# Backward of log-softmax: thirty-two groups in straight code, against two groups and a loop of fifteen rounds

## The chip, the cores and the metric

The kernel runs on one core of a Trainium2 chip. The metric is the device time of one execution in microseconds, median of several. All runs told here were at a granted clock of 1.0; executions of one kernel mostly lie within 0.1% of one another. SyncE issues all transfers, ACT (ScalarE) and DVE (VectorE) compute.

## The reference, cut to what matters

```python
y, dy: float32 [8, 1024, 8192]
softmax_x = np.exp(y)
sum_dy = np.sum(dy, axis=-1, keepdims=True)
return (dy - softmax_x * sum_dy).astype(np.float32)
```

## The kernel before

8192 rows are taken in 32 groups of 128 partitions x 2 rows, so a group is 128 x 16384 floats, 8.39 MB, and a partition's part of it is one run of 64 KiB. Two dy buffers (x0, x1) and one y buffer that two groups share with an offset hold two groups at a time; groups therefore go in pairs A, B. The Python loop unrolls to straight code. The part that matters:

```python
    def sums(j):                       # -sum(dy) of both rows: one on DVE, one on ACT
        ...
    def compute(j, at, pieces, in_psum):
        for b, e in pieces:
            ...                        # ACT: exp of a piece of y, in place or into PSUM
            ...                        # DVE: x = exp * (-sum) + x, in place

    for g in range(0, G, 2):
        load_dy(g, 0)                  # dy A -> x0
        load_y(g, SHIFT)               # y A
        sums(0)
        compute(0, SHIFT, EXP_A, (IN_PSUM, IN_PSUM + Q))
        load_dy(g + 1, 1)              # dy B -> x1
        sums(1)
        load_y(g + 1, 0)               # y B, over most of y A
        store(g, 0, 0, W)              # store A
        for r in range(R):
            compute(1, 0, EXP_B[3 * r : 3 * r + 3], ())
            store(g + 1, 1, r * D, (r + 1) * D)   # store B, in two halves
```

## Time and profile before

| | before |
|---|---|
| time, median | 1867.8 us |
| span in the profile | 1865.8 us |
| bytes moved / mean rate | 805.31 MB / 432 GB/s |
| transfers' share of 16 DMA engines | 99.8% |
| DVE / ACT busy | 46% / 37% |
| dy load, issue to landing (median) | 47.9 us |

The lines for these stand in the prediction. A transfer of 8.39 MB needs 19.4 us at this rate, yet takes 47.9 us from issue to landing: the difference is time in the queue. One further pair of lines is needed below, from the timeline of the kernel before at its very start (start us, duration us): the only moment at which a load meets an empty queue.

```profile
0.73 0.38 SPq L61 DMA_DIRECT2D x<-in_dy_dram  x1
...
22.50 8.69 DVE L72 TENSOR_REDUCE stats<-x 128x1 f32<-128x8192 f32 x1 [22.50 <-DMA x<-in_dy_dram]
```

It was issued at 0.73 and had landed at 22.50: 21.8 us, 2.4 us more than its bytes need.

### The profile page before, as it was taken

The numbers are of one execution on the slowest core, as the hardware profiler recorded it, in microseconds if no ns is written. First come the engines' busy times: TensorE is split into PE (matmuls) and PEld (weight loads), VectorE is DVE, ScalarE is ACT, GpSimd is POOL, SyncE is SP. The second block draws the span as 40 slices with busy tenths as digits, with TensorE's granted clock in tenths as the row PEclk, the third lists the DMA queues.
The fourth block names the chain that finished last, engine by engine and source line by source line (L and its number), as shares of the span: only waits on it lengthen the run. The fifth ranks groups of instructions, "written<-read, shape, count | busy, mean of one in ns | idle before, by whom it ended". The sixth has DMA issues, their size and how long they took to land.

```text
span 1865.8 us, 920 instructions
## 1 busy us (share of the span) xinstructions
DVE 860.6 (46%) x288; ACT 689.0 (37%) x273; POOL 0.2 (0%) x4
## 2 busy tenths in 40 slices
DVE  2717427173271732717327173271733716337163
ACT  2606326053260532605326053260533605335053
POOL 0000000000000000000000000000000000000000
DMA  9999999999999999999999999999999999999998
GB/s 427 427 427 427 433 444 427 431 444 421 435 441 434 429 430 441 430 430 441 430 431 440 431 432 434 436 430 431 441 430 430 436 436 431 433 440 426 433 437 377
DMA packets 16135, 805.37 MB, mean 432 GB/s; under 512 B 1792, under 2 KB 1792, under 8 KB 1792
## 3 DMA queue, kind: packets, MB, share of 16 engines
q1 hardware_dynamic: 16128, 805.31, 99.8%
q14 instruction: 7, 0.06, 0.0%
HBM read 536.87 MB, written 268.44 MB: 432 GB/s over the span
## 4 chain that ended last, share of the span: by engine, by line
DMA 56%; DVE 18%; ACT 12%; another core or an unknown queue 10%; issue 2%; SPq 0%; ACTq 0%; DVEq 0%
DMA x<-in_dy_dram 30%; DMA y_t<-in_y_dram 26%; DVE x L96 18%; ACT y_t L92 6%; ACT x L75 6%; SPq L67 0%; ACTq L142 0%; DVEq L142 0%; SPq L61 0%; SPq L64 0%; ACTq L92 0%; ACTq L75 0%
## 5 line engine op out<-in xcount | busy, mean ns | idle before, releaser
L96 DVE SCALAR_TENSOR_TENSOR x<-y_t,stats,x 128x1024 f32<-128x1024 f32 (+2 forms) x192 | 511.1, 2704 | 396.1 <-ACT y_t L92 394.7
L72 DVE TENSOR_REDUCE stats<-x 128x1 f32<-128x8192 f32 x32 | 277.9, 8683 | 589.9 <-DMA x<-in_dy_dram 589.9
L92 ACT ACTIVATE y_t<-y_t 128x3072 f32<-128x3072 f32 (+6 forms) x176 | 403.7, 2362 | 393.6 <-DMA y_t<-in_y_dram 393.6
L75 ACT ACTIVATE x<-x 128x8192 f32<-128x8192 f32 x32 | 225.0, 7030 | 757.4 <-DMA x<-in_dy_dram 732.8
L96 DVE SCALAR_TENSOR_TENSOR x<-e_t,stats,x 128x2048 f32<-128x2048 f32 x32 | 73.7, 2345 | 0.0
L92 ACT ACTIVATE e_t<-y_t 128x2048 f32<-128x2048 f32 x32 | 58.5, 1858 | 0.0
L75 ACT ACTIVATION_READ_ACCUMULATOR x<-x 128x1 f32 x32 | 6.0, 187 | 0.0
L76 DVE TENSOR_SCALAR stats<-stats 128x1 f32<-128x1 f32 x32 | 4.6, 145 | 0.0
L75 ACT ACT_TABLE_LOAD x1 | 1.3, 1283 | 0.7 <-PEq L131 0.7
L131 POOL MEMSET const-bfloat16-1.0<- 128x1 bf16 x1 | 0.1, 102 | 0.0
L131 POOL MEMSET const-uint8-127<- 128x1 uint8 x1 | 0.1, 101 | 0.0
L131 POOL MEMSET const-float32-0.0<- 128x1 f32 x1 | 0.1, 99 | 0.2 <-issue 0.2
L131 POOL MEMSET const-float32-1.0<- 128x1 f32 x1 | 0.1, 98 | 0.0
## 6 DMA issues: line engine op xcount, KB each, us to landing
out_dram<-x SPq DMA_DIRECT2D x32, 4096.0 KB, 18.3
x<-in_dy_dram SPq DMA_DIRECT2D x32, 47.9
y_t<-in_y_dram SPq DMA_DIRECT2D x32, 34.6
out_dram<-x SPq DMA_DIRECT2D x16, 38.2
```

Source lines behind the costliest of these rows:

```text
L72: nc.vector.tensor_reduce(out=stats[:, c : c + 1], in_=x[:, :D], axis=mybir.AxisListType.X, op=ALU.add, negate=True)
L75: nc.scalar.activation(x[:, D:], x[:, D:], COPY, accum_out=stats[:, c + 2 : c + 3])
L76: nc.vector.tensor_scalar(out=stats[:, c + 1 : c + 2], in0=stats[:, c + 2 : c + 3], scalar1=-1.0, scalar2=None, op0=ALU.mult,)
L92: nc.scalar.activation(e_ap, y_t[:, at + b : at + e], EXP)
L96: nc.vector.scalar_tensor_tensor(out=x[:, lo:hi], in0=e_ap[:, lo - b : hi - b], scalar=stats[:, 4 * j + r : 4 * j + r + 1], in1=x[:, lo:hi ...
L131: nc = _bacc.Bacc("TRN2", target_bir_lowering=False, num_devices=1)
```

## The change

The intent is a short program at the same speed: the first pair stays straight code, the other fifteen are rounds of one loop. The loop resets its semaphores stage by stage, so that engines need not all meet at the branch (a barrier there instead made it 1935.2 us and not 1867.6, as run barrier shows below). The author cut the loop body into four stages, lets ACT and DVE report a stage finished at the start of the next one (`done_early`), and declares the three stores independent, since with a register in the address the compiler can't see it.

```diff
-    for g in range(0, G, 2):
-        load_dy(g, 0)
-        load_y(g, SHIFT)
+    def done_early():
+        for engine in (mybir.EngineType.Activation, mybir.EngineType.DVE):
+            tc.previous_stage_wait(engine)
+
+    def two_groups(h, boundary, early):
+        load_dy(h, 0)
+        load_y(h, 0, SHIFT)
+        boundary()
+        early()
         sums(0)
         compute(0, SHIFT, EXP_A, (IN_PSUM, IN_PSUM + Q))
-        load_dy(g + 1, 1)
+        load_dy(h, 1)
+        boundary()
+        early()
         sums(1)
-        load_y(g + 1, 0)
-        store(g, 0, 0, W)
-        for r in range(R):
-            compute(1, 0, EXP_B[3 * r : 3 * r + 3], ())
-            store(g + 1, 1, r * D, (r + 1) * D)
+        load_y(h, 1, 0)
+        compute(1, 0, EXP_B, ())
+        boundary()
+        stores = [store(h, 0, 0, W), store(h, 1, 0, D), store(h, 1, D, W)]
+        for k, later in enumerate(stores):
+            for earlier in stores[:k]:
+                tc.declare_no_dep(later.ins, earlier.ins, reason="different parts of out")
+
+    two_groups(0, lambda: None, lambda: None)
+    with tc.For_i(1, G // 2, 1, iteration_sync="staggered") as h:
+        two_groups(h, tc.stage_boundary, done_early)
```

(The cut parts give the views of y, dy and out a second index for A and B.)

More of the change, by code (lines that the diff above doesn't have):

```diff
@@ L47 @@
     assert D <= IN_PSUM
-    y_v = y.flatten_outer_dims().rearrange("(g p r) d -> g p (r d)", p=P, r=R)
-    dy_v = dy.flatten_outer_dims().rearrange("(g p r) d -> g p (r d)", p=P, r=R)
-    out_v = out.flatten_outer_dims().rearrange("(g p r) d -> g p (r d)", p=P, r=R)
+    y_v = y.flatten_outer_dims().rearrange("(h j p r) d -> h j p (r d)", j=2, p=P, r=R)
+    dy_v = dy.flatten_outer_dims().rearrange("(h j p r) d -> h j p (r d)", j=2, p=P, r=R)
+    out_v = out.flatten_outer_dims().rearrange("(h j p r) d -> h j p (r d)", j=2, p=P, r=R)
     pool = ctx.enter_context(tc.tile_pool(name="pool", bufs=1))
@@ L58, with load_dy, load_y, store @@
     stats = pool.tile([P, 8], fp32, name="stats")
-    def load_dy(g, j):
-        nc.sync.dma_start(out=x_ts[j][:], in_=dy_v[g])
-    def load_y(g, at):
-        nc.sync.dma_start(out=y_t[:, at : at + W], in_=y_v[g])
-    def store(g, j, lo, hi):
-        nc.sync.dma_start(out=out_v[g][:, lo:hi], in_=x_ts[j][:, lo:hi])
+    def load_dy(h, j):
+        nc.sync.dma_start(out=x_ts[j][:], in_=dy_v[h, j])
+    def load_y(h, j, at):
+        nc.sync.dma_start(out=y_t[:, at : at + W], in_=y_v[h, j])
+    def store(h, j, lo, hi):
+        return nc.sync.dma_start(out=out_v[h, j][:, lo:hi], in_=x_ts[j][:, lo:hi])
     def sums(j):
```

## The prediction

> **What bounds the kernel now.** I read four views in this order: the busy rows of the page, the list of transfers, what the transfer-issuing queue waited for, and one pair of groups on the timeline.
>
> The busy rows and the slices come first (engine, busy us, share, instructions; then the mean busy share and rate of the 16 DMA engines in 40 slices).
>
> ```profile
> span 1865.8 us, 920 instructions
> DVE 860.6 (46%) x288; ACT 689.0 (37%) x273; POOL 0.2 (0%) x4
> ...
> DMA  9999999999999999999999999999999999999998
> DMA packets 16135, 805.37 MB, mean 432 GB/s; under 512 B 1792, under 2 KB 1792, under 8 KB 1792
> q1 hardware_dynamic: 16128, 805.31, 99.8%
> ```
>
> The reader is to see that neither compute engine passes half the span while the DMA engines are busy 99.8% of it. 805.31 MB is the least that can move: three tensors of 8 x 1024 x 8192 x 4 = 268.4 MB, two read and one written. At 432 GB/s that is 1864 us of the 1866. So nothing can be gained except by a higher rate, and a loss needs one thing only: a moment when the transfer queue is empty.
>
> The question is therefore how much transfer work is still queued whenever SyncE issues the next transfer. One group of 128 x 16384 floats is 8.39 MB, 19.4 us at 432 GB/s; half a group is 9.7 us. Here is SyncE's issuing over one steady pair (start us, duration us, line, operation; L61 loads dy, L64 loads y, L67 stores):
>
> ```profile
> 916.06 0.33 SPq L67 DMA_DIRECT2D out_dram<-x  x1
> 916.44 0.77 SPq L61 DMA_DIRECT2D x<-in_dy_dram  x1
> 917.30 0.73 SPq L64 DMA_DIRECT2D y_t<-in_y_dram  x1
> 934.45 0.33 SPq L61 DMA_DIRECT2D x<-in_dy_dram  x1
> 984.32 0.33 SPq L64 DMA_DIRECT2D y_t<-in_y_dram  x1
> ```
>
> and from the same stretch of the compute engines' timeline, when data landed (the end of the idle time in brackets is the landing):
>
> ```profile
> 953.80 7.03 ACT L75 ACTIVATE x<-x 128x8192 f32<-128x8192 f32 x1 [43.71 <-DMA x<-in_dy_dram]
> ...
> 973.15 7.36 ACT L92 ACTIVATE y_t<-y_t 128x1024 f32<-128x1024 f32 x4 [12.23 <-DMA y_t<-in_y_dram]
> ...
> 993.13 39.79 SPq L67 DMA_DIRECT2D out_dram<-x  x3
> ...
> 1012.29 14.32 ACT L92 ACTIVATE y_t<-y_t 128x2048 f32<-128x2048 f32 x6 [12.68 <-DMA y_t<-in_y_dram]
> ```
>
> Landings are 953.7, 973.1, about 992.5 (ACT begins the next sum then) and 1012.3: one every 19.4 us, back to back. From that I get the slack of each issue, i.e. how much later it could come before the queue ran dry:
> - y of the second group, issued 984.3; what is ahead of it lands at 992.5: slack **8.2 us**.
> - store of the first group, issued 993.1; y ahead of it lands 1012.3: 19 us.
> - the two half stores: issued 907.1 and 916.1 in the pair shown. The y ahead landed at 897.6 and the three stores were all down by 934.4 (when the dy load of L61 that needs the second buffer was let go), 36.8 us for two groups' worth, so the first group's store ended near 916.0 and the first half near 925.2: slack **8.9 and 9.1 us**.
> - next dy and y, issued 916.4 and 917.3, stores ahead to 934.4: 18 us, and more for y.
> - dy of the second group, issued 934.45; dy and y ahead to 973.1: 39 us.
>
> The queue's waits confirm which work lets these go:
>
> ```profile
> SPq L64 <- DVE x L96: 793.1, 16, 50.9
> SPq L67 <- DVE x L96: 748.7, 48, 30.7
> SPq L61 <- DMA out_dram<-x: 246.8, 17, 17.2
> ```
>
> SyncE waits nearly all the time, and that is harmless, because it always waits with at least 8 us of work queued.
>
> [...]
>
> **The change, part by part.**
> Transfers: same bytes, same 64 KiB runs for loads (a partition's 16384 floats), same 64 and 32 KiB runs for stores. SyncE's order is the same too: dy A, y A, dy B, y B, store A, store B low, store B high. Compute instructions and their shapes are the same. Worth: 0.
>
> The store calls move in the text behind all the compute of the second group. On SyncE's own queue they were already behind the y load; a store still needs only the pieces it carries, so "store B low" may go out at mid compute as before, provided SyncE has been let into the last stage by then. Worth: 0 if so.
>
> Each of 15 rounds adds a branch, register address arithmetic (seven transfers) and four stage entries. As I read the loop's stages: an engine enters a stage only when its own work, transfers included, of the stage two back is complete and every other engine has reported the same. Taken on the old times:
> - entering the stage with y B (needed by 984.3) asks for dy A and y A landed: 973.1. Free by 11 us. DVE and ACT report early, at the start of their stage, not after computing A at 993.1.
> - entering the stage with the stores (993.1) asks for dy B landed, 992.5, and compute A ended, 993.1. DVE and ACT report that at the start of the next stage; without the early report it would be at the end of compute B, 1032.5, 20 us after the queue ran dry at 1012.3.[...]
> - the round's start (916.4) asks for y B landed (897.6) and compute B ended (916.0)[...].
> - entering the stage with dy B asks for all stores landed (934.4). The old dy B load waited for just that.
> Thus each added wait ends at or before an old one[...]. On the path: **0 us per round**.
>
> Once only, on entering the loop from the straight code, I expect SyncE to wait for the straight code's stores to land before the first load of the loop. The queue then empties once. What an empty queue costs is seen at the start: the first dy load is issued at 0.73 us and landed at 22.50, 21.8 us for 19.4 us of bytes, so 2.4 us.[...] Sum: 1867.8 + 5 = 1872.8; I shade it to **1871**, since the entry may turn out free.
>
> **The rivals.**
> (1) Each round starts with an empty queue, because the loop's first dy load is made to wait for all three stores instead of only the first. Then 2.4 us[...] recur 15 times: 51 us, 1919 us, slower by 2.7%. For it: waits across a loop's branch are easily made coarse. Against it: the two dy buffers are separate tiles, and the author untied the stores from one another. One in nine.
> (2) A stage report comes late, and y B or the stores go out after the queue is dry: from 1 to 20 us per round, 1880 to 2170 us. For it: the smallest slack is only 8.2 us. Against it: the early reports are there for this. A few in a hundred.
> [...]
> (4) A gain, from fewer instructions or a better mix of reads and writes: the busy row leaves 0.2%, and the order of transfers is the same. One in a hundred.
>
> **Range and chances.** The middle is one drained queue, 1871. The lower end, 1866, is a free entry; the upper, 1888, allows about 1 us per round on top (15 us) and the entry. The threshold for slower, 1905, needs 2.5 us lost per round, which only (1) and (2) give: 12%. Faster: 1%. Within 2%: 87%.
>
> **What would show it.** In the changed kernel's profile the DMA share should stay 99% with the row of nines, and the mean rate at 430 GB/s or more. At the first entry one gap of up to 5 us; at the other rounds none. The y B load should still be held by DVE, and the first dy load issued within 3 us of the last half store, well before the stores land. Landings should stay 19.4 us apart. DVE and ACT busy times should not change. I would be wrong if the dy load of the round's start waits for the last stores' landing (rival 1: a dip in the busy row each 116 us), if the stores go out together after compute B, or if another number of packets appears[...].

Passages that no trace of this case shows are cut, as marked, and their terms are still in the sums. The sum for entering and leaving the loop came to 5 us, hence 1867.8 + 5 = 1872.8, shaded to 1871; only the 2.4 us of the empty queue are measured, and the other terms guesses. Rival 1's 51 us came to 3.4 us a round; again 2.4 us are measured and the rest a guess. The guess for a round's own bookkeeping is cut too; the trace taken after the change shows it: the gap from last store to next load grew by 0.8 us, of 18 us of slack.

## The result, and the profile after

After: 1867.6 us median (1866.96 to 1867.91, 4 runs); before beside it 1867.9 (1867.36 to 1868.62). The ratio is 0.9998, 95% interval 0.998 to 1.0015: the same. (A ratio is the mean time of one kernel's runs over that of the other's of the same rounds, so not quite the ratio of the medians quoted.)

From the page of the changed kernel, the lines that answer to the first ones of the prediction:

```profile
span 1866.1 us, 2175 instructions
...
DVE 861.9 (46%) x288; ACT 689.0 (37%) x273; POOL 0.2 (0%) x4
...
DMA  9999999999999999999999999999999999999998
...
DMA packets 16129, 805.32 MB, mean 432 GB/s; under 512 B 1792, under 2 KB 1792, under 8 KB 1792
...
q1 hardware_dynamic: 16128, 805.31, 99.8%
q14 instruction: 1, 0.01, 0.0%
```

Recorded instructions rise from 920 to 2175 (waits, register and branch instructions of the stages), and nothing else moves: busy times, packets and share are those of before. The last line is the queue that carries instructions: one packet, where the page of before has seven. By the trace it came at 1865.7 us, the very end, so none came in any round of the loop.

SyncE's issues over one round of the changed kernel (L62 loads dy, L65 loads y, L68 stores):

```profile
916.36 0.33 SPq L68 DMA_DIRECT2D out_dram<-x  x1
917.52 0.35 SPq L62 DMA_DIRECT2D x<-in_dy_dram  x1
918.12 0.60 SPq L65 DMA_DIRECT2D y_t<-in_y_dram  x1
935.32 0.33 SPq L62 DMA_DIRECT2D x<-in_dy_dram  x1
984.92 0.33 SPq L65 DMA_DIRECT2D y_t<-in_y_dram  x1
994.05 38.87 SPq L68 DMA_DIRECT2D out_dram<-x  x3
```

From the end of the last store's issue (916.69) to the next load's start (917.52) now pass 0.83 us; before it was 0.05 us (916.39 to 916.44). In that gap lie SyncE's stage entry, the branch and the addresses. The load still goes out 17.8 us before the last store has landed (935.32, when the load that waits for it is let go). The same at the entry from the straight code:

```profile
92.98 9.25 SPq L68 DMA_DIRECT2D out_dram<-x  x2
103.62 0.36 SPq L62 DMA_DIRECT2D x<-in_dy_dram  x1
104.24 0.45 SPq L65 DMA_DIRECT2D y_t<-in_y_dram  x1
120.68 0.33 SPq L62 DMA_DIRECT2D x<-in_dy_dram  x1
```

The stores' issue ends at 102.23, the first load of the loop follows 1.4 us later, 17 us before the stores have landed. The waits in the compiled program say why (an instruction listing, not a profile; the names are the compiler's semaphores):

```
L62 DMACopy x_61<-in_dy_dram 128x16384 [waits DMAHW7_49,DMAHW4_49]
...
L62 ISA [waits DMAHW0_49,DMAHW1_49,DMAHW7_49,sem_stage_3_181]
L62 DMACopy x_62<-in_dy_dram 128x16384 [waits DMAHW6_49,DMAHW5_49]
```

The round's first load waits for store A alone, that of the round before (7) and that of the straight code (4). All three stores of a round (0, 1, 7) are waited for only at the entry of the stage that holds the dy B load, which needs them down anyway.

What SyncE waited for in all (us in total, times, longest):

```profile
SPq L68 <- DVE x L97: 610.5, 33, 30.5
SPq L131 <- DMA y_t<-in_y_dram: 568.3, 15, 37.9
SPq L131 <- DMA out_dram<-x: 226.4, 28, 10.0
SPq L65 <- DVE x L97: 213.4, 16, 51.1
SPq L131 <- DMA x<-in_dy_dram: 114.9, 15, 7.7
```

L131 is the loop's line: these are the stage entries, about 910 us of new waiting. It was carved out of the old waits (L65 fell from the 793 us of its counterpart to 213) and costs nothing, because it too is spent with transfers queued.

### The profile page after: what moved, and what is told of

The parts are those of the page before. It is cut to its first block, busy times and chain, and to the rows that moved or that the text cites. A ratio compares the mean times of both kernels' runs of the same rounds, so it can differ in the third digit from the quotient of the medians.

```text
span 1866.1 us, 2175 instructions
## 1 busy us (share of the span) xinstructions
DVE 861.9 (46%) x288; ACT 689.0 (37%) x273; POOL 0.2 (0%) x4
## 3 DMA queue, kind: packets, MB, share of 16 engines
q1 hardware_dynamic: 16128, 805.31, 99.8%
## 4 chain that ended last, share of the span: by engine, by line
DMA 51%; DVE 15%; ACT 11%; another core or an unknown queue 10%; issue 5%; SPq 1%; ACTq 0%
DMA x<-in_dy_dram 29%; DMA y_t<-in_y_dram 22%; DVE x L97 15%; ACT x L76 6%; ACT y_t L93 5%; SPq L68 0%; SPq L131 0%; ACTq L93 0%; SPq L65 0%; SPq L62 0%; SPq L158 0%; ACTq L131 0%; ACTq L76 0%
```

## The experiments

Twelve runs. The first eleven edit the changed kernel, the last one the kernel before. "Round" is one pair of groups; a loop has fifteen, the program sixteen. A first overview, with the loss per round worked out as time less that of before, divided by the rounds edited:

| run | time, us | before beside it | loss per round, us |
|---|---|---|---|
| late_a | 1878.7 | 1868.4 | 0.7 |
| late_b | 2123.8 | 1868.4 | 17.0 |
| tied_stores | 1940.6 | 1868.4 | 4.8 |
| drained_round | 1928.5 | 1868.4 | 4.0 |
| barrier | 1935.2 | 1868.4 | 4.5 |
| slow_report_8192 | 1867.9 | 1868.4 | 0 |
| slow_report_16384 | 1907.3 | 1868.4 | 2.6 |
| delay_4096 | 1886.1 | 1868.0 | 1.1 |
| delay_8192 | 1927.4 | 1868.0 | 3.7 |
| delay_12288 | 2065.4 | 1868.0 | 12.3 |
| no_straight | 1868.9 | 1868.0 | (0.9 once) |
| late_half | 1882.9 | 1868.2 | 1.8 |

### Is the slack at the round's start real, and is the stage report what lets SyncE in?

```diff
         compute(1, 0, EXP_B, ())
+        if early is done_early:        # rounds of the loop only
+            nc.vector.tensor_reduce(
+                out=junk[:], in_=x_ts[1][:, :8192], axis=mybir.AxisListType.X, op=ALU.add
+            )
```

and the same with 16384 columns (`junk`, one column of scratch, is declared in a line cut here, as in the runs with delays below). Nobody needs the result; only DVE's report of the stage comes later.

> In each round of the loop DVE sums 8192 extra columns (8.7 us) after computing B, inside the third stage, whose result nobody needs. Only the stage report comes later: SyncE may not begin the next round before DVE has finished. Slack theory: the round's first load comes 8.7 us later, of 18 us of slack, and costs nothing: 1868 us. Rival (the report is not what lets SyncE in): also 1868 us, but then the first load of a round is still issued about 1 us after the last store; with the theory about 9 us after it.

> As before with 16384 columns, 17.4 us. Slack theory: the load goes out 17.4 + 0.8 us after the last store, when the queue has about 18 us; 2.4 us are needed to take effect, so about 2.5 us lost per round, 15 rounds 38 us: 1905 us, 2% slower. Rival (the report is not what lets SyncE in, or the rate alone counts): 1868 us.

With 8192 columns: 1867.9 us, ratio 0.9998 (0.9981 to 1.0014). With 16384: 1907.3 us, ratio 1.0212 (1.0194 to 1.0229). The timeline of the first, then of the second, from the last store of a round to the next load:

```profile
1032.54 0.33 SPq L69 DMA_DIRECT2D out_dram<-x  x1
1041.64 0.35 SPq L63 DMA_DIRECT2D x<-in_dy_dram  x1
```

```profile
932.45 0.33 SPq L69 DMA_DIRECT2D out_dram<-x  x1
950.21 0.35 SPq L63 DMA_DIRECT2D x<-in_dy_dram  x1
```

The load moved from 1.2 us to 9.1 and 17.8 us after the store. So the report does hold SyncE, a delay of about 8 us is free, and about 17 us passes the edge and costs 2.6 us per round where 2.5 was expected. This shows directly that the stages' waits are there and are hidden. That the second number came so near is partly luck: by the trace the load still went out 0.65 us before the stores had landed, and 1.8 us were lost there; another 1.0 us went at y B's landing, on slow packets that are told of below and that the expectation did not have.

### The round that starts with an empty queue (rival 1 of the prediction)

```diff
+        if early is done_early:
+            nc.sync.dma_start(out=x_ts[1][:, W - 64 :], in_=dy_v[h, 1][:, W - 64 :])
         load_dy(h, 0)
```

> A tiny load (64 columns of dy into the end of the second dy buffer, overwritten later by the full load) is put ahead of each round's first dy load; it must wait until the last store of the round before has landed, so each round starts with an empty queue: rival (1) of the prediction, alone. Slack theory: 2.4 us[...], 15 times: 36 to 44 us, 1904 to 1912 us, 2.0 to 2.4% slower. The prediction's estimate for the same was 3.4 us a round, 1919 us. Rival (rate alone): 1868 us.

(The 44 us hold a term for the small transfer besides the 2.4 us; no trace had shown it.)

1928.5 us, ratio 1.0323 (1.0305 to 1.034): the cost is 4.0 us per round, more than expected. The timeline shows the tiny load (L113) waiting for the stores and the real one going out behind it:

```profile
944.40 0.33 SPq L68 DMA_DIRECT2D out_dram<-x  x1
962.90 0.35 SPq L113 DMA_DIRECT2D x<-in_dy_dram  x1
963.51 0.35 SPq L62 DMA_DIRECT2D x<-in_dy_dram  x1
```

The dy load landed at 985.57, so 22.7 us after the tiny one went out, 3.3 us over the 19.4 of its bytes: 2.4 us of an empty queue, 0.6 us for SyncE's second issue, and some 0.3 for the small transfer. The remaining 0.7 us or so appears later in the round, at the landing of y B; it is taken up below. Note what the page shows of this run:

```profile
DMA  9999999999999999999999999999999999999999
...
q1 hardware_dynamic: 18288, 805.81, 98.1%
```

The row of nines hides fifteen drained queues; only the share, 98.1% instead of 99.8%, gives them away.

### A full barrier at the branch

```diff
-    with tc.For_i(1, G // 2, 1, iteration_sync="staggered") as h:
-        two_groups(h, tc.stage_boundary, done_early)
+    with tc.For_i(1, G // 2, 1, iteration_sync="barrier") as h:
+        two_groups(h, lambda: None, lambda: None)
```

> The same loop with a full barrier of all engines at each round's end instead of staged resets; the stage boundaries and early reports go. SyncE has to wait for every transfer to land before the next round. Slack theory: an empty queue (2.4 us) and the barrier's own handshake[...] 15 times: 58 to 81 us, 1926 to 1949 us, 3 to 4.3% slower. Rival (rate alone): 1868 us. A loss no greater than that of the run with the drained round would mean that the barrier itself is free.

(The 58 to 81 us are 3.9 to 5.4 us a round: the measured 2.4 us of an empty queue, and a guess for the handshake, which no trace had shown.)

1935.2 us, ratio 1.0357 (1.034 to 1.0375), 4.5 us per round, inside the expected span. The barrier costs 0.5 us a round more than the drained queue alone, which contained some 0.9 us of its own for the tiny load. So the barrier's handshake is about 1.4 us of it at most, and most of its price is the empty queue that it brings. The trace has the same number directly: the first load of a round goes out 1.4 us (median) after the last store has landed. This is what the staged resets save.

### Stores that wait for one another

```diff
-        for k, later in enumerate(stores):
-            for earlier in stores[:k]:
-                tc.declare_no_dep(later.ins, earlier.ins, reason="different parts of out")
```

> The three declarations that the stores of a round are independent are removed, so each store of the loop waits for the one before it to have landed. Slack theory: SyncE issues the second and third store of a round to an empty queue, twice 2.4 us per round, 15 rounds 72 us: 1940 us, 3.9% slower. Rival (the stores follow one another on one queue anyway, so the wait is hidden): 1868 us.

1940.6 us, ratio 1.0386 (1.0369 to 1.0404), as expected in sum. In parts it was less neat. The trace records when all 16 engines have reported a transfer's end; from these the two half stores of a round took 11.2 and 12.2 us instead of 9.7, so 1.5 and 2.5 us lost, and y B 20.4 us instead of 19.35 (medians). Two drained queues did not cost 2.4 us each, and a third term made up the sum.

### Reports that come late

Run late_a leaves out `early()` at the start of the second stage, run late_b that at the start of the third:

```diff
         boundary()
-        early()
         sums(0)        # late_a;  sums(1) in late_b
```

> Only the early report at the start of the second stage is removed: ACT and DVE then report the first stage at the end of computing A, and SyncE may issue y B only after that. Slack theory (a late issue costs only what it lies beyond the end of the queued work, and a queue that ran empty costs 2.4 us more, as the first load showed): y B goes out at about 993.3 instead of 984.3 on the old clock, the work ahead of it is down at 992.5, so 0.8 + 2.4[...] = 3.7 us per round, 15 rounds 55 us: 1923 us, 2.9% slower. Rival (the transfer rate alone sets the time, order and waits are of no account): 1868 us. Rival (each wait costs what it is moved, 9 us a round): 2003 us.

> Only the early report at the start of the third stage is removed: SyncE enters the stage with the stores only after ACT and DVE have computed B. Slack theory: store A goes out at about 1033 instead of 993.1 on the old clock; the work ahead of it is down at 1012.3, so 20.7 + 2.4 = 23 us per round, 15 rounds 346 us: 2214 us, 18.5% slower. Rival (rate alone): 1868 us. Rival (each wait costs what it is moved, 40 us): 2468 us.

(The 3.7 us expected of late_a hold a term for the handshake besides 0.8 and 2.4 us; it was a guess.)

Both lost less than expected: 10 us, ratio 1.0052 (1.0031 to 1.0072), and 255 us, ratio 1.1367 (1.1348 to 1.1386). The timeline of late_b, at y B's landing (998.35) and the stores:

```profile
998.35 14.32 ACT L93 ACTIVATE y_t<-y_t 128x2048 f32<-128x2048 f32 x6 [12.14 <-DMA y_t<-in_y_dram]
1000.35 2.35 DVE L97 SCALAR_TENSOR_TENSOR x<-y_t,stats,x 128x2048 f32<-128x2048 f32 x1 [12.01 <-ACT y_t L93]
1002.95 15.67 DVE L97 SCALAR_TENSOR_TENSOR x<-y_t,stats,x 128x3072 f32<-128x3072 f32 x5 [0.25 <-ACT y_t L93]
1013.10 5.87 SPq L68 DMA_DIRECT2D out_dram<-x  x3
```

The stores were let go at 1013.10, 0.4 us after ACT's last exp (1012.67), and not after DVE's last piece (1018.62). So the two engines' reports were in by the end of ACT's work, 14.75 us after y B's landing, where I had taken the end of DVE's, 20.7. Why DVE's report did not wait for its last piece is not shown. With that one term put right the sum of the slack rule is exact: 14.75 + 2.4 = 17.15 us, and the period of a round grew from 116.25 to 133.4 us, 17.15 us. (It is exact as a sum: of the 2.4 us, the landings show about 1.5 at store A and 1.0 at the last half store.) The same in late_a: y B went out at 988.59, which is 0.6 us after ACT's last exp of A and 3.7 us later than in the changed kernel relative to y A's landing, not 9. Of the 8.2 us of slack it used less than half, and still it lost something. Why is the question of the next runs.

### How much delay of y B is free?

```diff
         for b, e in pieces:
+            if j == 0 and b == 1024:
+                nc.vector.tensor_reduce(
+                    out=junk[:], in_=x[:, :4096], axis=mybir.AxisListType.X, op=ALU.add
+                )
```

with 4096, 8192 and 12288 columns.

> DVE sums 4096 extra columns (about 4.35 us, from 8.69 us for 8192) in the middle of computing A, in every round, so y B and store A are issued that much later. y B has 8.2 us of slack, of which 2.4 us is the time an issue needs to take effect: 5.8 us are free. Slack theory: 4.35 us is within it, 1868 us, same. Rival (any delay of an issue adds up): 16 x 4.35 = 70 us, 1938 us.

> As before with 8192 columns, 8.69 us: 8.69 - 5.8 = 2.9 us beyond the slack, 16 times 46 us: 1914 us, 2.5% slower. If the issue needs no time to take effect (slack 8.2 us): 8 us in all, 1876 us. Rival (any delay adds up): 2007 us.

> As before with 12288 columns, 13.0 us: 13.0 - 5.8 = 7.2 us beyond the slack, 16 times 115 us: 1983 us, 6.2% slower; between this and the run with 8192 columns the loss should grow by the whole added 4.35 us per round. Rival (any delay adds up): 2076 us.

Times 1886.1, 1927.4 and 2065.4 us; ratios 1.0101 (1.0086 to 1.0116), 1.0321 (1.0305 to 1.0336) and 1.1056 (1.104 to 1.1073). First the sizes. Measured from y A's landing, y B was issued 15.3, 19.35 and 27.95 us later instead of 11.2, so the delays were really 4.0, 8.1 and 16.7 us. The last is larger than the added 13.0, because the compiler there put a piece of 4032 columns ahead of the pieces that y B still waits for. From the timeline of that run:

```profile
944.80 12.95 DVE L90 TENSOR_REDUCE junk<-x 128x1 f32<-128x12288 f32 x1
...
957.67 12.46 DVE L102 SCALAR_TENSOR_TENSOR x<-y_t,stats,x 128x4032 f32<-128x4032 f32 x5
...
970.05 4.60 DVE L102 SCALAR_TENSOR_TENSOR x<-e_t,stats,x 128x2048 f32<-128x2048 f32 x2
970.28 0.33 SPq L66 DMA_DIRECT2D y_t<-in_y_dram  x1
```

With delays of 8.1 and 16.7 us the rule (delay less 8.2 plus 2.4) gives 2.3 and 10.9 us; measured were 3.7 and 12.3, in both 1.4 us more. With 4.0 us it gives 0, measured was 1.1 on average, and not evenly. Periods of the rounds, from one start of ACT's first exp of B to the next, in us:

```
changed   116.1 116.1 116.3 116.2 116.5 116.2 117.0 116.2 116.2 116.2 116.2 116.2 116.2 116.2 116.2
4096      116.2 116.4 116.1 116.5 116.2 116.2 117.4 117.9 118.1 118.4 118.1 118.1 117.7 117.9 117.6
late_a    116.1 116.1 116.2 116.7 116.4 116.3 116.6 116.1 119.0 117.7 117.7 118.0 117.7 117.7 117.5
8192      120.0 120.4 120.1 120.0 119.9 120.2 120.0 120.1 119.8 119.9 120.2 119.9 119.8 120.0 120.2
```

The two runs with short delays keep the full speed for six to eight rounds and then lose 1.2 to 2.8 us in each. (Their executions also differ more than those of any other run, 1882.4 to 1888.6 us and 1874.0 to 1882.3, and one of each was traced.) Something fills up over the execution. The trace has two candidates. First, each transfer's end is reported by 16 engines one by one; how far the first and last report lie apart, in us, mean over a round's transfers:

```
                2nd round   8th   16th
before            0.6       2.6   5.0
changed           0.6       2.6   4.6
tied_stores       0.7       0.6   0.6
barrier           0.9       0.6   0.7
```

In these runs the engines drift apart as long as the queue never drains, and where it drains every round they stay lined up. The foremost engine then has so much less slack than the last one. The trace lets this be checked round by round: the foremost engine's slack is the time from y B's issue to the first of the 16 reports that dy B has landed. In the seven runs whose queue is meant never to drain (before, changed, no_straight, slow_report_8192, late_a, 4096 and late_half, which is told below; rounds 2 to 16 of each) it was 0.65 to 1.94 us in 23 rounds, and in these y B took 20.7 to 21.6 us; in the other 82 it was 2.6 us or more, and y B took 19.3 to 20.4. The split lies about where an issue to an empty queue would put it, at 2.4 us: the loss comes when the foremost engine runs dry.

Second, a packet of 64 KiB takes 2.418 us in the median, but in the rounds that lose, and in most rounds that follow a drained queue, the last packets of y B, just ahead of the stores, 16 in number, as many as there are engines, take 3.3 to 3.7 us on average. Run late_b is the exception: its queue is empty for 14.8 us in every round of the loop, but between y B and the stores, so that no store is queued when y B lands, and none of these rounds has a slow packet. In the changed kernel this is seen in full only in the straight-code pair (16 packets over 2.9 us), in all its other rounds together there are five; in run 8192 it is 16 in every round, in run 4096 16 or 17 from the ninth on. 3.6 less 2.4 is 1.2 us per round, nearly the 1.4 us that the rule lacks in the two long delays and about the last us in the drained round.

### Does the drift explain it, or the number of delayed rounds?

The kernel before, straight code, with the sum of 4096 columns in its last eight pairs alone:

```diff
-        compute(0, SHIFT, EXP_A, (IN_PSUM, IN_PSUM + Q))
+        compute(0, SHIFT, EXP_A, (IN_PSUM, IN_PSUM + Q), late=g >= G // 2)
```

> The straight-code kernel of before, with the extra sum of 4096 columns (as in the run with 4096 columns) in its last 8 pairs of groups only. In that run the first 6 rounds kept the full speed although each was delayed by 4 us, and the later ones lost about 1.7 us each, while the 16 DMA engines' reports of one transfer's end had drifted from 0.6 us apart to over 2 us. Theory A: the foremost engines run dry because engines drift apart as long as the queue never drains, delay or no delay; then the last 8 pairs lose from the first or second of them on, 8 x 1.1 to 1.7 = 9 to 14 us, 1877 to 1882 us. Theory B: it takes some 6 delayed rounds before a loss begins, wherever they stand; then only the last 2 pairs lose, 3 us, 1871 us.

1882.9 us, ratio 1.0077 (1.0064 to 1.0091), just over the span of theory A and far from that of B. The periods:

```
late_half 116.2 116.8 116.8 116.4 116.3 116.6 116.1 118.4 118.0 118.1 117.8 118.0 118.0 118.2 117.9
```

The loss begins with the first delayed pair. In run 4096 the early rounds bore the same delay without loss. So position in the execution decides, which fits the drift (2.8 us in this run by then) and rules out a count of delayed rounds; and it happens without a loop. The foremost engine's slack fell from 5.2 us in the pair before to 1.2 in the first delayed one. Three things stay open. A place in the execution is in every run also a place in the tensors, and no run takes the groups in another order, so a rival by address is not excluded. The drift is not the same with and without a delay, as theory A had it: in the seventh round it was 2.0 us in the changed kernel and 0.9 in run 4096. And what makes the packets ahead of the stores slow is not shown: there are 16 or 17 of them, also where the engines are 3 us apart, and no run isolates it.

### Is the straight-code pair worth anything?

```diff
-    two_groups(0, lambda: None, lambda: None)
-    with tc.For_i(1, G // 2, 1, iteration_sync="staggered") as h:
+    with tc.For_i(0, G // 2, 1, iteration_sync="staggered") as h:
```

> The two groups of straight code are removed and the loop runs 16 rounds from the start. Theory: entering the loop costs SyncE 1.4 us (store's issue to the next load, traced) against 0.05 us of straight code, and here nothing is queued to hide it: about 1 to 1.5 us, once, 1869 us, same. Rival (the straight code saves a drained queue or more): 2.4 us or more, 1870 us and up.

1868.9 us, ratio 1.0004 (0.999 to 1.0017): no difference can be told. The timeline has the first load at 2.03 us instead of 0.74, and the table load of ACT now in every round (16 in all, 1.28 us each):

```profile
2.03 0.40 SPq L62 DMA_DIRECT2D x<-in_dy_dram  x1
2.63 0.35 SPq L65 DMA_DIRECT2D y_t<-in_y_dram  x1
3.37 1.28 ACT L76 ACT_TABLE_LOAD   x1 [3.37 <-issue]
```

The pair hides 1.3 us of entering the loop, which is what the trace gives and the medians (0.9 us) don't contradict; the table loads, 20.5 us in sum, are hidden in any case.

No variant beat the two kernels: with the engines busy 99.8% of the time there is next to nothing left to win at this rate.

## Why the prediction was right

The verdict, same, and its reason held: every added wait ended while transfers were queued. Point by point.

**Cost per round, 0: right.** The gap from last store to next load grew by 0.8 us and dissolved in 18 us of slack. Run slow_report_8192 put 8 us more there for nothing, and slow_report_16384 found the edge where the slack put it.

**Entering the loop and leaving it, 5 us in the sum: wrong in size, both nil within the noise.** The failed step is "I expect SyncE to wait for the straight code's stores to land before the first load of the loop". The waits across the loop's edge are kept per buffer; the load went out after 1.4 us of bookkeeping, with 17 us queued. Hence 1867.6 us where 1871 was predicted.

**Early reports: right that they matter, wrong in when a late one comes.** The estimate took the report of computing B at DVE's end. It comes with ACT's, 14.75 us after y B's landing and not 20.7, so late_b lost 17 us a round.

**Rival 1, 3.4 us per drained round, 1919 us: a little small.** Its own run measured 4.0 us and 1928.5; what lacked is mainly the slow last packets of y B. It would have been "slower", as was said. But the sign named for it, a dip in the busy row, does not exist: the row stays at nines.

**A slip in reading.** The prediction takes 897.6 as y B's landing in the pair shown. That was the start of ACT's second exp; the window had cut off the first. The timeline of the kernel before has the landing here:

```profile
895.76 4.56 ACT L92 ACTIVATE y_t<-y_t 128x2048 f32<-128x2048 f32 x2 [12.13 <-DMA y_t<-in_y_dram]
```

So the three stores took 38.7 us and not 36.8, no faster than loads, and the half stores' slacks were about 8 and 8.7 us instead of 8.9 and 9.1. The verdict didn't rest on it.

**Slack counted on the last engine alone: an omission.** "It always waits with at least 8 us of work queued" holds for the engine that reports last. By the end of an execution the first is 4.6 to 5 us ahead: in the last round it had 3.5 us left of y B's 8.2 (2.6 in the kernel before), against the 2.4 that an issue to an empty queue costs, so only about 1 us was free there. Delays of 3.7 and 4.0 us already cost time. The loop moved y B's issue by only 0.1 us, so this smaller margin was not put to the test; that part of the hit is luck.

## What to carry to other kernels

In a kernel bound by transfers, price a new wait by the work still queued when it ends, not by its length: here 910 us of new waiting cost nothing, while a queue drained at each of 15 rounds cost 4.0 to 4.5 us every time. Here the loop was as fast as straight code (1867.6 against 1867.9 us): its waits across the branch stayed per buffer, and no engine's report was later than the slack allowed, where late_b's, which was, cost 17 us a round. Check the latter at each stage entry, and keep some us in hand, since the DMA engines drifted apart (from 0.6 to 5 us over an execution). Read the share of the DMA queue and not the row of tenths, which was all nines in drained_round, with fifteen drained queues and a share of 98.1%.
